# High and low parts of a 16-column weight side by side in one stationary tile

## The chip, the cores and the metric

The program runs on one core of a Trainium2 chip. The metric is the device time of one execution in microseconds (us), less is better. The core's engines work side by side, each through its own instructions in order: TensorE (PE in the rows; PEld are its weight loads), VectorE (DVE), ScalarE (ACT), GpSimd (POOL) and SyncE (SP, which here issues most transfers).

## The reference, cut to what matters

One inference step of a two-layer network for 640 tokens (128 of a prompt, 512 of a sample), all in float32. Each layer feeds a normalised input `h` to four token mixers, merges their outputs through gates, and ends with a feed-forward part. The first mixer is a gated delta rule. Its log decay `g` and write strength `beta` come from 16 columns of the input projection, 8 for the decay and 8 for the strength (2 directions x 4 heads):

```
aq, ak, av, az, aa, ab, ... = split(h @ w_in)           # aa, ab: 8 columns each
g    = -exp(a_log) * softplus(aa + dt_bias)
beta = sigmoid(ab)
o, state = chunked delta rule(q, k, v, g, beta, s0)
```

## The kernel before, in words

Activations stand with the features on the partitions and the 640 tokens along the row, in two halves of 320. To keep float32 accuracy, a matrix product of weights W and activations X is made from parts in the type fp32r: W = Wh + Wl and X = Xh + Xl, and the product is Wh Xh + Wh Xl + Wl Xh. `load_w` loads a weight tile (`wraw`), copies it to its high part `whi` on ScalarE and subtracts on VectorE to get the low part `wlo`. `unit` then makes one product for one half of the tokens: 8 blocks of 128 features, three matmuls each, summed in one PSUM bank `pu`. The activations' parts are `hh` and `hl`.

`a_small` is the projection to the 16 columns: one `load_w` of 128 columns (8 blocks of 16) and two `unit`s with M=16, that is 48 matmuls, whose result goes to `ab` (16 partitions x 640 tokens). `a_small2` turns `ab` with five PE transposes into `pabt` (tokens on the partitions), copies that to `abt` and computes decay and strength from it; `peg` are its small float32 matmuls.

The order of the work in the mixer stage of a layer is made by a planner in the program (`weave`). It has chains (the mixers, `prep_a`, `prep_b`, in a fixed order of rank) and fill (`a_small` first, then the other projections `store_fm` and `store_tok`, pregates and merges). It keeps a modelled clock, `self.now`, which each matmul moves on by its modelled cost; a chain's next step is put into PE's queue as soon as the modelled time of what it waits for, plus a margin, has come, and fill is put in between. PE keeps exactly that order. The orders of the other engines come from priorities and from the order in which the instructions were written.

Names in the rows: `cacc`, `craw` are the short convolution of `prep_a` (VectorE, six instructions a time); `pkS`, `xp`, `vn`, `pao` belong to the delta rule; `cY`, `cZ`, `cQS`, `cRP`, `pca`, `pcb`, `cAT` to the seven levels of `mix_c`, in which VectorE makes `cY` and `cZ` and PE multiplies them into `pca` and `pcb`; `rx`, `rr`, `rot` to the rotation in `prep_b`; `stg`, `sth` are the results of `store_fm` and their high parts on the way out to memory; `lmr`, `lmn` a small scalar of `mix_b`. `stg` and `sth` share six buffers, and three PSUM banks hold the fill's `pu`.

Of the kernel before, what the change touches and what calls it, by code (L numbers as in the profile page):

```python
# [8 lines left out]
F32 = mybir.dt.float32  # L9
F32R = mybir.dt.float32r  # L10
I32 = mybir.dt.int32
ACT = mybir.ActivationFunctionType
ALU = mybir.AluOpType
# [5 lines left out]
HT = T // 2  # L19
# [49 lines left out]
def bc1(ap, n):  # L69

    d = [list(x) for x in ap.ap]
    return bass.AP(tensor=ap.tensor, offset=ap.offset, ap=[d[0], [0, n]] + d[1:])
# [40 lines left out]
class Net:  # L113
# [600 lines left out]

    def a_small(self, l):

        w = self.load_w(self.I['wab'][l], 128)
        ab = self.S("ab")
        for j in range(2):
            ps = yield from self.unit(w, self.h, range(8), j, M=16)  # L720
            self.a.copy(ab[:16, j * HT:(j + 1) * HT], ps[:16, :HT])
        self.abT = ab
        self.ev['ab'] = self.now

    def a_small2(self, l):

        v, a = self.v, self.a
        yield 'ab',
        ab = self.abT
        yield ab,  # L730
        pt = self.M("pabt")
        for t in range(5):
            self.tp(pt[:, t * 16:(t + 1) * 16], ab[:16, t * 128:(t + 1) * 128], self.ident[:16, :16])
        abt = self.Q("abt", 80)
        v.tensor_copy(abt, pt[:, :80])
        abv = abt.rearrange("p (t c) -> p t c", t=5)
        f = lambda n: self.Q(n, 40)
        u, e, w1, r, d = f("a_u"), f("a_e"), f("a_w"), f("a_r"), f("a_d")
        q = lambda t: t.rearrange("p (t c) -> p t c", t=5)
        v.tensor_tensor(q(u), abv[:, :, 0:8], bc1(self.dtb[:, l, :], 5), ALU.add)  # L740
        a.activation(e, u, ACT.Abs)
        a.activation(e, e, ACT.Exp, scale=-1.0)
        v.tensor_scalar(w1, e, 1.0, None, ALU.add)
        a.activation(r, w1, ACT.Ln)
        v.tensor_scalar(d, w1, -1.0, 1e-30, ALU.add, ALU.max)
        v.reciprocal(d, d)
        v.tensor_tensor(r, r, e, ALU.mult)
        v.tensor_tensor(r, r, d, ALU.mult)
        v.scalar_tensor_tensor(u, u, 0.0, r, ALU.max, ALU.add)
        g = self.sm("a_g", 40)  # L750

        gv = g.rearrange("p (d t h) -> p t d h", d=2, t=5)
        ea = self.sm("a_ea", 8)
        a.activation(ea, self.alog[:, l, :], ACT.Exp)
        v.tensor_scalar(ea, ea, -1.0, None, ALU.mult)
        for dr in range(2):
            v.tensor_tensor(gv[:, :, dr], q(u)[:, :, dr * 4:dr * 4 + 4], bc1(ea[:, dr * 4:dr * 4 + 4], 5), ALU.mult)
        be = self.sm("a_b", 40)
        bv = be.rearrange("p (d t h) -> p t d h", d=2, t=5)
        for dr in range(2):  # L760
            a.activation(bv[:, :, dr], abv[:, :, 8 + dr * 4:12 + dr * 4], ACT.Tanh, scale=0.5)
        v.tensor_scalar(be, be, 0.5, 0.5, ALU.mult, ALU.add)
        yield g,
        pe = self.M("peg")
        for i, (m, dr) in enumerate(((self.Ui, 0), (self.Ls, 0), (self.ones, 0), (self.Li, 1), (self.Us, 1), (self.ones, 1))):
            self.mm(pe[:, i * 20:(i + 1) * 20], m, g[:, dr * 20:(dr + 1) * 20], start=True, stop=True)
        eg = self.sm("a_eg", 120)
        a.activation(eg, pe[:, :120], ACT.Exp)
        ng = self.sm("a_ng", 120)
        v.tensor_scalar(ng, eg, -1.0, None, ALU.mult)  # L770
        self.g_, self.be, self.eg, self.ng = g, be, eg, ng
# [1183 lines left out]
```

## Time and profile before

| | |
|---|---|
| median of 3 runs | 3432.06 us (3429.37 to 3438.22) |
| profiled execution: its own time | 3430.03 us |
| its span, first to last instruction | 3428.3 us |
| PE busy | 3344.3 us, 98% of the span, 23932 matmul records |
| VectorE, ScalarE, GpSimd busy | 68%, 41%, 6% |
| granted PE clock, mean | 0.992 of full speed |

PE is busy nearly all the time; its matmuls overlap, so their step (from one start to the next) tells their cost, not the mean duration. Two other things can lengthen the time: moments in which PE stands still, and stretches in which its clock is granted at less than full speed.

### The profile page before, as it was taken

The numbers are of one execution on the slowest core, as the hardware profiler recorded it, in microseconds if no ns is written. First come the engines' busy times: TensorE is split into PE (matmuls) and PEld (weight loads), VectorE is DVE, ScalarE is ACT, GpSimd is POOL, SyncE is SP. The second block draws the span as 40 slices with busy tenths as digits, with TensorE's granted clock in tenths as the row PEclk, the third lists the DMA queues.
The fourth block names the chain that finished last, engine by engine and source line by source line (L and its number), as shares of the span: only waits on it lengthen the run. The fifth ranks groups of instructions, "written<-read, shape, count | busy, mean of one in ns | idle before, by whom it ended". The sixth has DMA issues, their size and how long they took to land. (4 is left out here: it accounts for less than half of the span.)

```text
span 3428.3 us, 62644 instructions
## 1 busy us (share of the span) xinstructions
PE 3344.3 (98%) x23932; PEld 3279.3 (96%) x23932; DVE 2315.9 (68%) x5237; ACT 1420.5 (41%) x3166; POOL 215.6 (6%) x385
## 2 busy tenths in 40 slices
PE   8999999999999999999999999999999999999998
PEld 5999999999999999999999999999999999999998
DVE  7689888876675577887456898777555656634335
ACT  5354545554443352222253455455444433422222
POOL 1000001210010000000001010012010100000000
PEclk9999999999999999999999999999999999999999
DMA  6544334865453444544234432348444325322222
GB/s 220 161 154 137 122 118 143 241 192 175 130 148 100 132 155 145 154 151 134 79 124 145 146 121 99 112 135 238 143 150 137 104 82 169 100 72 76 75 80 68
DMA packets 288133, 460.10 MB, mean 134 GB/s; under 512 B 47061, under 2 KB 174677, under 8 KB 287833
## 3 DMA queue, kind: packets, MB, share of 16 engines
q1 hardware_dynamic: 276504, 423.58, 39.5%
q0 software_dynamic: 11328, 32.52, 3.2%
q8 instruction: 189, 3.10, 0.4%
q14 instruction: 112, 0.91, 0.1%
HBM read 368.42 MB, written 87.56 MB: 133 GB/s over the span
## 5 line engine op out<-in xcount | busy, mean ns | idle before, releaser
L151 PE MATMUL pu<-hh,whi 128*128 128x320 f32 (+1 forms) x3760 | 1090.7, 318 | 12.9 <-ACT stg L106 9.7
L151 PE MATMUL pu<-hl,whi 128*128 128x320 f32 (+1 forms) x3760 | 1061.8, 310 | 2.4 <-DVE hl L106 2.4
L151 PE MATMUL pu<-hh,wlo 128*128 128x320 f32 (+1 forms) x3760 | 1062.4, 310 | 0.0
L106 ACT CAST whi<-wraw 128x1024 fp32r<-128x1024 f32 (+2 forms) x410 | 390.4, 952 | 884.8 <-PE pu L151 562.4
L151 PEld LDWEIGHTS pu<-hh,whi 128*128 128x128 f32 (+1 forms) x3760 | 681.3, 188 | 17.7 <-ACT stg L106 10.5
L151 PEld LDWEIGHTS pu<-hl,whi 128*128 128x128 f32 (+1 forms) x3760 | 681.3, 188 | 4.5 <-DVE hl L106 2.6
L151 PEld LDWEIGHTS pu<-hh,wlo 128*128 128x128 f32 (+1 forms) x3760 | 680.0, 188 | 1.7
L106 DVE TENSOR_TENSOR wlo<-wraw,whi 128x1024 fp32r<-128x1024 f32 (+2 forms) x410 | 455.4, 1111 | 311.7 <-ACT whi L106 302.7
L151 PE MATMUL pu<-mo,whi 128*128 128x320 f32 x1024 | 233.9, 316 | 3.8 <-ACT mo L106 1.9
L151 PE MATMUL pu<-fa,whi 128*128 128x320 f32 x1152 | 215.6, 309 | 0.0
L106 DVE SCALAR_TENSOR_TENSOR x<-pu,gn,x 128x128 f32<-128x128 f32 (+1 forms) x336 | 134.0, 434 | 92.8 <-PE pu L151 91.8
L151 PE MATMUL ptk<-whi,hh 128*128 128x256 f32 x640 | 191.1, 299 | 0.0
L151 PE MATMUL ptk<-wlo,hh 128*128 128x256 f32 x640 | 181.1, 283 | 1.2 <-DVE wlo L106 1.2
L151 PE MATMUL ptk<-whi,hl 128*128 128x256 f32 x640 | 181.2, 283 | 0.0
L151 PEld LDWEIGHTS pu<-fa,whi 128*128 128x128 f32 x1152 | 180.8, 188 | 0.0
L151 PEld LDWEIGHTS pu<-mo,whi 128*128 128x128 f32 x1024 | 172.1, 190 | 5.8 <-DVE mo L106 3.1
L151 PE MATMUL pu<-mo,wlo 128*128 128x320 f32 x512 | 159.5, 311 | 0.0
L151 PE MATMUL pu<-fa,wlo 128*128 128x320 f32 x576 | 131.2, 309 | 0.0
L511 DVE CUSTOM_DVE_ANT_0 junk<-wa,cs,bada 128x512 bf16<-128x512 f32 x160 | 119.6, 747 | 7.1 <-DMA wa<-in_wada 4.8
L511 DVE CUSTOM_DVE_ANT_0 junk<-wa,cs,mod 128x512 bf16<-128x512 f32 x160 | 119.5, 747 | 7.0 <-DMA wa<-in_wada 4.6
L151 PEld LDWEIGHTS ptk<-wlo,hh 128*128 128x128 f32 x640 | 122.4, 191 | 1.4 <-DVE wlo L106 1.4
L106 DVE TENSOR_TENSOR fs<-fs,pu 128x320 f32<-128x320 f32 x88 | 39.6, 483 | 124.3 <-PE pu L151 124.3
(422 smaller groups left out, 5967.1 us busy)
## 6 DMA issues: line engine op xcount, KB each, us to landing
wraw<-in_win SPq DMA_DIRECT2D x151, 512.0 KB, 3.7
wa<-in_wada SPq DMA_DIRECT2D x180, 256.0 KB, 3.0
wraw<-in_wg SPq DMA_DIRECT2D x44, 512.0 KB, 3.5
wraw<-in_wu SPq DMA_DIRECT2D x44, 512.0 KB, 3.5
wraw<-in_wd SPq DMA_DIRECT2D x80, 256.0 KB, 2.6
p<-stg SPq DMA_DIRECT2D x112, 160.0 KB, 2.7
wraw<-in_wtok SPq DMA_DIRECT2D x32, 512.0 KB, 3.8
wraw<-in_wbr SPq DMA_DIRECT2D x32, 512.0 KB, 3.5
```

Source lines behind the costliest of these rows:

```text
L106: r = f(*args, **kw)
L151: r = self.nc.tensor.matmul(out, lhsT, rhs, start=start, stop=stop)
L511: self.nc.vector.tensor_tensor_reduce(junk, raw, cs[g], 0.5, o if k0 else self.bada[:, l, m:m + 1], ALU.mult, ALU.add, o)
```

## The change

`a_small` no longer makes two tiles. It copies the 8 blocks of 16 columns to places 0 to 15 of 32 columns per block, and writes the low part of the same block into places 16 to 31. A matmul with this 32-column tile gives the high part's product in 16 rows of the result and the low part's in 16 others, so that one block needs two matmuls (`hh` and `hl`) where it needed three; the product Wl Xl is now made too. `ab` has 32 partitions. `a_small2` builds a 32 x 16 matrix `two` (two identity matrices on top of each other) and replaces each transpose by a float32 matmul with it, which transposes and adds the two halves. The cast and the subtraction no longer have the raised priority that `load_w` gives them, and no `wlo` buffer is taken.

```diff
     def a_small(self, l):

-        w = self.load_w(self.I['wab'][l], 128)
+        raw = self.wraw.tile([128, 1024], F32, tag="raw", name="wraw")[:, :128].rearrange("p (k c) -> p k c", c=16)
+        self.nc.sync.dma_start(raw, self.I['wab'][l].rearrange("p (k c) -> p k c", c=16))
+
+        w = self.whl.tile([128, 1024], F32R, tag="hi", name="whi")[:, :256].rearrange("p (k c) -> p k c", c=32)
+        self.a.copy(w[:, :, :16], raw)
+        self.v.tensor_tensor(w[:, :, 16:], raw, w[:, :, :16].bitcast(F32), ALU.subtract)
         ab = self.S("ab")
         for j in range(2):
-            ps = yield from self.unit(w, self.h, range(8), j, M=16)
-            self.a.copy(ab[:16, j * HT:(j + 1) * HT], ps[:16, :HT])
+            ps = self.G1("pu")
+            c = slice(j * HT, (j + 1) * HT)
+            for k in range(8):
+                for i in range(2):
+                    self.mm(ps[:32, :HT], w[:, k], self.h[k][i][:, c], start=k == 0 and i == 0, stop=k == 7 and i == 1)
+                yield ()
+            self.a.copy(ab[:32, c], ps[:32, :HT])
...
         ab = self.abT
-        yield ab,
+        two = self.Q("two", 16)[:32]
+        v.tensor_tensor(two, self.ident[:32, :16], self.ident[:32, 16:32], ALU.add)
+        yield ab, two
         pt = self.M("pabt")
         for t in range(5):
-            self.tp(pt[:, t * 16:(t + 1) * 16], ab[:16, t * 128:(t + 1) * 128], self.ident[:16, :16])
+            self.mm(pt[:, t * 16:(t + 1) * 16], ab[:32, t * 128:(t + 1) * 128], two, start=True, stop=True)
```

In each layer PE's queue loses 16 matmuls. Because the planner's modelled clock is earlier by their cost from there on, it puts many later steps into PE's queue with a few matmuls of fill more or fewer between them. The three places below are those that matter for what follows.

Place 1 is PE in layer 0, the end of `a_small`; the fill behind it is the next `store_fm`. Before, the last rows with 16 columns and the transposes:

```order
L151 MATMUL pu<-hh,whi 16x320
L151 MATMUL pu<-hl,whi 16x320
L151 MATMUL pu<-hh,wlo 16x320
L151 MATMUL pu<-hh,whi 128x320
L151 MATMUL pu<-hl,whi 128x320
L151 MATMUL pu<-hh,wlo 128x320
L157 MATMUL pabt<-cst_119,ab 128x16 x5
```

The same place after the change:

```order
L151 MATMUL pu<-hh,whi 32x320
L151 MATMUL pu<-hl,whi 32x320
L151 MATMUL pu<-hh,whi 128x320
L151 MATMUL pu<-hl,whi 128x320
L151 MATMUL pu<-hh,wlo 128x320
L151 MATMUL pabt<-two,ab 128x16 x5
```

One matmul of three is gone from each block, 48 rows of this kind have become 32 in each layer; `pabt` stands as many rows behind them as it did.

Place 2 is VectorE in layer 1, first head of `mix_c`, the rows that end with the `cZ` of the sixth level. Before:

```order
L106 SCALAR_TENSOR_TENSOR cacc<-craw,convw,cacc 128x642
L106 SCALAR_TENSOR_TENSOR SS<-SS,a_eg,pkS 128x128
L106 SCALAR_TENSOR_TENSOR cacc<-craw,convw,cacc 128x642
L106 SCALAR_TENSOR_TENSOR xp<-pkS,a_ng,avt 128x128
L106 SCALAR_TENSOR_TENSOR cacc<-craw,convw,cacc 128x642
L106 SCALAR_TENSOR_TENSOR xp<-pkS,a_ng,avt 128x128
L106 TENSOR_TENSOR cY<-cY,cK 128x640
L106 TENSOR_SCALAR vn<-pkS,a_b 128x128 x2
L106 SCALAR_TENSOR_TENSOR cacc<-craw,cacc 128x642
L106 TENSOR_TENSOR wlo<-wraw,whi 128x1024
L106 TENSOR_TENSOR cZ<-cZ,cq 128x640
```

After the change the rows that end with the same `cZ` are these:

```order
L106 TENSOR_SCALAR ars_y<-ars_t 128x5
L106 SCALAR_TENSOR_TENSOR xp<-pkS,a_ng,avt 128x128
L106 SCALAR_TENSOR_TENSOR ars_t<-ars_y 128x5
L106 TENSOR_TENSOR GX<-GX,pX 128x4x2x64
L106 TENSOR_TENSOR ars_t<-ars_t,ams 128x5
L106 SCALAR_TENSOR_TENSOR xp<-pkS,a_ng,avt 128x128
L106 SCALAR_TENSOR_TENSOR ars_y<-ars_t,ars_y 128x5
L106 TENSOR_TENSOR cY<-cY,cK 128x640
L106 TENSOR_TENSOR ars_t<-ars_y,ams 128x5
L106 COPY_PREDICATED cAT<-cst,pca 128x512
L106 SCALAR_TENSOR_TENSOR ars_t<-ars_t,ars_y 128x5
L106 TENSOR_TENSOR cZ<-cZ,cq 128x640
```

Between the fifth level's `cZ` and this one there stood six convolution rows and three `wlo` of 1024 columns; now there is neither.

Place 3 is VectorE in layer 1, where `mix_b` begins and four `stg` wait for their low part (`stg<-stg,sth`). Before:

```order
L106 TENSOR_TENSOR cZ<-cZ,cq 128x640
L106 TENSOR_TENSOR cRP<-cRP 128x10x2x32
L106 TENSOR_TENSOR cY<-cY,cK 128x640
L106 TENSOR_TENSOR cQS<-cQS,cRP 128x5x2x64
L106 TENSOR_TENSOR lmn<-lmr 128x1
L106 TENSOR_TENSOR rx<-rx,rr 128x2x512
L106 TENSOR_TENSOR wlo<-wraw,whi 128x1024
L106 TENSOR_TENSOR cQS<-cQS,cK 128x640 x2
L106 TENSOR_SCALAR lmn<-lmn 128x1
L106 TENSOR_TENSOR stg<-stg,sth 128x192
L106 TENSOR_TENSOR stg<-stg,sth 128x320
L106 TENSOR_TENSOR stg<-stg,sth 128x192
```

After the change:

```order
L106 TENSOR_REDUCE lmr<-lmp 128x2
L106 TENSOR_TENSOR rr<-rr,rot 128x2x512
L106 TENSOR_TENSOR lmn<-lmr 128x1
L106 TENSOR_TENSOR stg<-stg,sth 128x320
L106 TENSOR_SCALAR lmn<-lmn 128x1
L106 TENSOR_TENSOR rx<-rx,rr 128x2x512
L106 TENSOR_TENSOR stg<-stg,sth 128x192
L106 TENSOR_TENSOR stg<-stg,sth 128x320
L106 TENSOR_TENSOR rx<-rx,rr 128x2x512
L106 TENSOR_TENSOR stg<-stg,sth 128x192
L106 COPY_PREDICATED cAT<-cst,pca 128x512
L106 COPY_PREDICATED cAT<-cst,pcb 128x128
```

The four subtractions stood behind the last levels of `mix_c` and now stand ahead of two more of them.

## Rows read from the trace of the kernel before

**Rows 1.** The page: span, and busy time of PE.

```profile
span 3428.3 us, 62644 instructions
PE 3344.3 (98%) x23932; PEld 3279.3 (96%) x23932; DVE 2315.9 (68%) x5237; ACT 1420.5 (41%) x3166; POOL 215.6 (6%) x385
```

**Rows 2.** Timeline of PE, layer 0: start us, duration us, instruction, [idle before].

```profile
69.00 0.31 PE L151 MATMUL pu<-hh,whi 128*128 128x320 f32 x1
...
69.89 0.31 PE L151 MATMUL pu<-hh,whi 128*16 128x320 f32 x1
70.03 0.30 PE L151 MATMUL pu<-hl,whi 128*16 128x320 f32 x1
...
76.92 0.32 PE L151 MATMUL pu<-hh,whi 128*128 128x320 f32 x1
...
77.46 0.48 PE L157 MATMUL pabt<-cst,ab 16*128 16x16 f32 x5
77.88 0.41 PE L151 MATMUL pu<-hh,whi 128*128 128x320 f32 x1
```

**Rows 3.** Weight loads by tile: minimum/median/maximum ns, and forms.

```profile
L151 PEld LDWEIGHTS pu<-hh,whi x3760: 94/188/337, 40.4 to 3368.4; 128*128 128x128 f32 x196, 128*16 128x16 f32 x2
L151 PEld LDWEIGHTS peg<-a_g,cst x24: 187/192/192, 86.7 to 1796.8; 128*128 128x128 f32 x24
```

**Rows 4.** Timeline of PE, layer 0: the six float32 matmuls of 20 columns.

```profile
86.89 1.41 PE L151 MATMUL peg<-a_g,cst 128*128 128x20 f32 x12
88.14 0.39 PE L151 MATMUL pu<-hh,whi 128*128 128x320 f32 x1
```

**Rows 5.** Timeline of VectorE: start of the program, and the low part in each layer.

```profile
3.00 0.17 DVE L106 TENSOR_SCALAR a_b<-bada 128x8 f32<-128x8 f32 x1 [3.00 <-DMA bada<-in_bada]
...
68.97 0.29 DVE L106 TENSOR_TENSOR wlo<-wraw,whi 128x128 fp32r<-128x128 f32 x1
...
1760.65 0.29 DVE L106 TENSOR_TENSOR wlo<-wraw,whi 128x128 fp32r<-128x128 f32 x1 [0.91 <-ACT whi L106]
```

**Rows 6.** Timeline of PE, layer 1: first 16-column product, and the transposes.

```profile
1777.86 0.31 PE L151 MATMUL pu<-hh,whi 128*16 128x320 f32 x1
...
1786.37 0.35 PE L157 MATMUL pabt<-cst,ab 16*128 16x16 f32 x3 [0.64 <-ACT ab L106]
```

**Rows 7.** Whom PE waited for: us in total, times, longest.

```profile
PE pu L151 <- ACT stg L106: 9.7, 3, 6.9
PE pca L151 <- DVE cZ L106: 8.0, 2, 4.4
```

**Rows 8.** Timeline around the longest pause: VectorE, ScalarE, PE.

```profile
2349.05 1.02 DVE L106 TENSOR_TENSOR stg<-stg,sth 128x192 fp32r<-128x192 f32 x3
2349.43 0.44 ACT L106 ACTIVATE stg<-pu 128x320 f32<-128x320 f32 x1 [2.81 <-DVE stg L106]
2349.92 0.63 PE L151 MATMUL pu<-hh,whi 128*128 128x320 f32 x1 [6.95 <-ACT stg L106]
```

**Rows 9.** Timeline around the second pause: VectorE, PE.

```profile
2014.07 0.83 DVE L106 SCALAR_TENSOR_TENSOR cacc<-craw,cacc 128x642 f32<-128x642 f32 x1 [0.30 <-ACT craw L106]
2014.81 1.22 DVE L106 TENSOR_TENSOR wlo<-wraw,whi 128x1024 fp32r<-128x1024 f32 x1
2015.95 1.67 DVE L106 TENSOR_TENSOR cZ<-cZ,cq 128x640 f32<-128x640 f32 x1
2017.76 2.04 PE L151 MATMUL pca<-cZ,cY 128*128 128x128 f32 x8 [4.42 <-DVE cZ L106]
```

**Rows 10.** Windows behind pauses: busy us of each engine, then PEclk, DMA share, GB/s.

```profile
2350.00:2356.00 6.00, 6.00 (x26) 6.00 (x27) 1.44 (x4) 1.93 (x7) 2.86 (x6) 0.53 1.03 282
2018.00:2024.00 6.00, 6.00 (x37) 5.99 (x38) 6.00 (x9) 2.34 (x8) 2.25 (x2) 0.74 0.16 61
656.00:660.00 4.00, 4.00 (x21) 4.00 (x20) 4.00 (x8) 3.64 (x8) 0.00 (x0) 0.60 1.07 287
```

**Rows 11.** Timeline of VectorE, layer 0: its longest wait at the rotation.

```profile
652.86 1.23 DVE L106 TENSOR_TENSOR rx<-rx,rot 128x1024 f32<-128x1024 f32 x1 [8.72 <-issue]
```

## The prediction, made before the changed kernel ran

> **What bounds the kernel.** I read the page first: PE is busy for 3344.3 of 3428.3 us [rows 1], so what PE has to do, and where it stands still, sets the end; the other engines matter only where PE waits for them. Then PE's timeline around `a_small`: its 48 products of 16 columns per layer run without a gap among the products of 128 columns, in the same step [rows 2]. They are on the path, each at its full step. Then the list of whom PE waited for [rows 7]. Few waits are long; the two longest are one of 6.9 us for an `stg` of ScalarE and one of 4.4 us for a `cZ` of VectorE. The timelines of those places [rows 8, 9] say what was late, and windows just behind them [rows 10] show the granted clock: 0.53 over 6 us after the first, 0.74 over 6 us after the second, so that PE, having stood still, worked for some us at the lower level of 1.2 GHz. A pause costs more than its own length.
>
> **The products.** In layer 0 the 48 products start at 69.89 us and the next 128-column product at 76.92 us [rows 2]: 7.03 / 48 = 0.1465 us each. The six 128-column products before them take (69.89 - 69.00) / 6 = 0.148 us each, so the number of columns in the stationary tile doesn't show in the step, and 32 should cost what 16 and 128 do. Sixteen fewer in each of two layers: 32 x 0.1465 = 4.7 us less. The bound on the other side: nothing in the rows lets a 32-column product be slower than a 128-column one, which would be 64 x 0.0015 = 0.1 us.
>
> The weight loads of `pu` take 94 to 337 ns, median 188 [rows 3], longer than the step, and the short loads of the 16-column tiles bring no shorter step: the loads lie under the matmuls. A rule of the Trainium skill (TensorE: Matmul & The Clock Gate, Part 3, The mechanism) speaks against that: a load overlaps with matmuls under way only where it goes to other row groups, and all tiles here fill all 128 rows. With that page's load time of columns / 1.2 ns (section on LDWEIGHTS), an estimate would be that each of the 64 remaining products has 13 ns more to load, 0.9 us in all. The equal steps don't agree with that rule.
>
> **The transposes.** Five transposes take from 77.46 to 77.88 us, 0.084 us each [rows 2]. Their place is taken by five float32 matmuls of 16 columns, a kind that the trace doesn't have in this shape. Nearest are the six `peg`, float32 with 20 columns: 86.89 to 88.14 us, 0.209 us each [rows 4], because each is recorded as two loads and two matmuls (24 loads for twelve of them, [rows 3]). Bounds: 0.084 and 0.209 us. I take the upper one, since the shape is almost the same: 10 x (0.209 - 0.084) = 1.25 us more in two layers. The Trainium skill (FP8 and Floating Point Precision, TensorE Precision Notes) says that true float32 takes four passes; the rows show two records each, and with twice the price the whole count would save some 1.3 us instead of 3.4.
>
> **What is hidden.** The low part is now written with stride into the same tile, and as all 32 columns are read at once, the first product must wait for it. In layer 0 it was ready at 68.97 + 0.29 = 69.26 us [rows 5] and the first product started at 69.89: 0.63 us of cover, over twice the instruction's length. If the strided write doubled its time, the first product would still not wait; if the cover were gone, it would cost at most 0.3 us, once. In layer 1 the cover is from 1760.94 to 1777.86 us [rows 5, 6]. Both instructions have kept their places in their queues although they lost priority. `two` costs a VectorE instruction of 0.17 us like `a_b` [rows 5]; in layer 0 it is VectorE's first, ahead of `a_b`, which waits until 3.00 us for a transfer that SyncE issues after the one `two` needs. The copies of `ab` have the same length along the row. In layer 1 the last transposes waited 0.64 us for `ab` [rows 6]; their place behind it is kept, so I let that wait stay, and bound it by 0 and 0.64. The chain behind `a_small` (decay, strength, `peg`) starts some 2 us earlier relative to the fill; PE has fill to do all the while, so nothing comes of that by itself.
>
> So the count alone gives 4.7 - 1.25 = 3.4 us less. Against the profiled execution's own time, 3430.0, that is 3426.6.
>
> **What is moved.** The planner's clock is 16 products earlier in each layer, and with that the rows of every engine in the mixer stages are shuffled a little. That is a change of PE's pauses, not of its work. The two longest pauses are the ones to look at.
>
> The longest: the fill's product waited 6.95 us for a PSUM bank; ScalarE could not empty it because it had no free `stg` buffer, as the `stg` ahead waited on VectorE for their subtraction, which began only at 2349.05 us [rows 8]. Place 3 shows why: they stood behind the last levels of `mix_c`, `rx` and a `wlo`. After the change four of them stand ahead of the next two levels. Price of the pause with the slower clock after it: 6.95 + 6 x 0.47 = 9.8 us.
>
> The second: `pca` waited 4.42 us because VectorE had the convolution and a `wlo` ahead of `cZ` [rows 9]. In place 2 both are gone from between these two levels. Price: 4.42 + 6 x 0.26 = 6.0 us.
>
> Bounds of what the two give back: 0 and 15.8 us. A row order says who stands ahead, not when an input comes, so I take six tenths, 9.4 us. New pauses must come up elsewhere from the same shuffle: bounds 0 and another 15.8; I take one of the third size, the other wait for `cZ`, 8.0 - 4.4 = 3.6 us [rows 7], with 4 x 0.40 = 1.6 us of clock behind it [rows 10]: 5.2 us. Sum: 3426.6 - 9.4 + 5.2 = 3422.4 us; I say **3422**. The profiled execution is 2 us under the median of the runs, 3432.06. A change of 0.3%, about what a measurement of this kernel can tell from none, is 10.3 us: below 3421.8 or above 3442.4.
>
> **The rivals.**
>
> *Only the count.* New pauses cost what the old ones did: 3426.6. For it: the pauses are many, most of them short, and a shuffle removes as readily as it adds. Against it: places 2 and 3. Chance 0.25.
>
> *Both pauses go and nothing comes up*: 3426.6 - 15.8 = 3410.8. For it: the same places; against it: every one of the later rows is moved, and none of those moves was chosen for its waits. Chance 0.14.
>
> *Slower, by VectorE standing at the rotation.* VectorE waits in its queue for a transfer at `rx`, the longest time 8.72 us [rows 11], and the levels of `mix_c` behind it wait too. Where the shuffle puts `rx` ahead of a level that PE needs at once, PE stands for up to 8.72 us, and with 2.8 us of clock as after the longest pause that is 11.5 us. One such more gives 3438, no difference that shows; it decides from two on: 3426.6 + 23 = 3450. Eight `rx` in the two layers could do it. Against it: in the rows of before the wait of 8.72 us cost PE only the 3.6 us one. Chance 0.09.
>
> *The count doesn't arrive*: 32-column products or the float32 ones cost so much more that nothing is saved: 3430. The equal steps speak against it. Chance 0.07.
>
> **How the numbers follow.** The forecast has 0.45, with its own range 3416 to 3428. It lies at the border of 0.3%, so half of it counts as faster. Faster: 0.22 + 0.14 + 0.04 of "only the count" = 0.40. Slower: 0.08 of the rotation's 0.09. Same: 0.52. The range 3409 to 3438 takes in the case without the two pauses and a single new long one, and leaves out the two-fold rotation and the far end of the best case, together under 2 in 10.
>
> **What would show it.** Right: 32 products in 4.7 us per layer between the neighbours; `pabt` in about 1.05 us; the wait of `pu` for `stg` well under 6.9 us and that of `pca` for `cZ` under 4.4 us; and the sum of PE's pauses smaller by some us. Wrong: a step over 0.15 us for the 32-column products; a gap ahead of the first of them; a new pause over 5 us, above all with VectorE waiting at `rx`; or windows with a granted clock near 0.5 in places that had 1.0.

## The result and the profile after

The changed kernel takes 3456.28 us (median of 6 runs, 3443.23 to 3461.32) against 3432.62 us (6 runs of the kernel before beside them): ratio 1.0065, 95% interval 1.0050 to 1.0081. It is slower by 24 us. The forecast was 3422, the range ended at 3438: the prediction was wrong, in sign too.

The profiled execution took 3453.77 us, 23.7 us more than that of before. The page of the changed kernel, to be read beside [rows 1]:

```profile
span 3452.0 us, 62597 instructions
PE 3354.9 (97%) x23910; PEld 3290.6 (95%) x23910; DVE 2315.5 (67%) x5239; ACT 1413.8 (41%) x3162; POOL 214.6 (6%) x385
```

PE has 22 matmul records fewer (32 products less, 10 records of `pabt` more) and is busy 10.6 us longer. That looks like a contradiction, until the granted clock is read with it: 0.988 as a mean, where it was 0.992. A rough split of the span follows from three numbers of each page. Time in which PE stands still is the span less PE's busy time: 84.0 us before, 97.1 after, 13.1 more. Time lost to the clock is at most span x (1 - clock): 27.4 and 41.4 us, 14 more (the clock has three digits, so each of the two is known to 1.7 us). What is left, PE's work at full clock, is 3316.9 and 3313.5: 3.4 us less. That it is just the 3.4 of the count is luck: in the profiles of the experiments below the same sum gives 3308 to 3317 for kernels with the changed kernel's very work. So the split says that the loss lies in pauses and in the clock; the saving of the count has to be read from PE's timeline.

That is, in layer 0, against [rows 2]:

```profile
66.80 0.30 PE L151 MATMUL pu<-hh,whi 128*32 128x320 f32 x1
66.94 0.30 PE L151 MATMUL pu<-hl,whi 128*32 128x320 f32 x1
...
71.49 0.32 PE L151 MATMUL pu<-hh,whi 128*128 128x320 f32 x1
...
72.60 1.28 PE L151 MATMUL pabt<-two,ab 32*128 32x16 f32 x10 [0.50 <-ACT ab L106]
73.81 0.41 PE L151 MATMUL pu<-hh,whi 128*128 128x320 f32 x1
```

The 32 products take from 66.80 to 71.49 us, 0.1466 us each where the 16-column ones took 0.1465. No gap stands ahead of the first. The weight loads of the 32-column tiles are recorded with 108 ns (median), those of the 16-column ones with 95, and the step doesn't show the difference. The estimate of 13 ns more for each product, by the rule of the Trainium skill (TensorE: Matmul & The Clock Gate, Part 3, The mechanism) with the load time of its section on LDWEIGHTS, is not borne out in the step. `pabt` takes 1.21 us to the next start, 0.242 us for each of the five, a little over the upper bound of 0.209; it waited 0.50 us for `ab`.

Now the waits. Whom PE waited for in the changed kernel (us in total, times, longest), against [rows 7]:

```profile
PE pco L151 <- DVE cSS L106: 9.3, 4, 3.7
PE pu L151 <- ACT stg L106: 9.0, 3, 4.8
PE pca L151 <- DVE cZ L106: 8.1, 2, 4.5
...
PE pcs L151 <- ACT ckd L106: 2.8, 2, 2.5
...
PE pat L157 <- DVE a_ea L106: 2.6, 1, 2.6
```

The two rows on which the gain was built (`pu` for `stg`, `pca` for `cZ`) stand nearly as before in their totals, 9.0 and 8.1 us where they were 9.7 and 8.0, and new names have come up. PE's timeline shows where (in the brackets the pause, and who ended it):

```profile
85.43 1.30 PE L157 MATMUL pat<-cst,cacc 128*128 128x128 f32 x5 [2.55 <-DVE a_ea L106]
...
609.92 0.38 PE L151 MATMUL pcs<-cv,ckd 128*128 128x128 f32 x1 [2.46 <-ACT ckd L106]
656.20 2.07 PE L151 MATMUL pca<-cZ,cY 128*128 128x128 f32 x8 [4.50 <-DVE cZ L106]
680.45 0.63 PE L151 MATMUL pu<-hh,whi 128*128 128x320 f32 x1 [3.82 <-ACT stg L106]
...
960.00 0.44 PE L157 MATMUL pds<-cst,dP 128*128 128x128 f32 x2 [2.53 <-ACT dP L106]
1993.02 1.72 PE L151 MATMUL pca<-cZ,cY 128*128 128x128 f32 x8 [3.58 <-DVE cZ L106]
...
2014.48 1.06 PE L151 MATMUL pca<-cZ,cY 128*128 128x128 f32 x8
...
2049.32 0.79 PE L151 MATMUL pco<-cSS,cRP 128*128 128x128 f32 x2 [3.26 <-DVE cSS L106]
2171.37 0.80 PE L151 MATMUL pco<-cSS,cRP 128*128 128x128 f32 x2 [3.65 <-DVE cSS L106]
2345.86 0.63 PE L151 MATMUL pu<-hh,whi 128*128 128x320 f32 x1 [4.76 <-ACT stg L106]
```

The reader is to see many pauses of 2.5 to 5 us, of different names and in both layers, and no single culprit. The row at 2014.48 is the sixth level of `mix_c` in the first head of layer 1, place 2 of the change: its wait of 4.42 us [rows 9] is gone, and the 3.58 us at 1993.02 are a new wait of the same kind two levels earlier. Over the whole timeline pauses of 2 us and more were 11, together 39.2 us, and are 17, together 54.7 us. Windows around three of the new ones (busy us of each engine, PEclk, DMA share, GB/s):

```profile
84.00:92.00 8.00, 6.57 (x28) 6.60 (x29) 2.38 (x11) 2.79 (x14) 0.16 (x3) 0.58 0.20 68
2046.00:2056.00 10.00, 6.74 (x34) 6.68 (x34) 4.81 (x10) 4.77 (x13) 1.98 (x3) 0.66 0.44 136
2170.00:2178.00 8.00, 6.63 (x45) 6.64 (x46) 2.70 (x7) 3.26 (x13) 1.17 (x1) 0.79 0.63 190
```

The granted clock was 0.58, 0.66 and 0.79 there, that is, a good part of each window at 1.2 GHz. In the first, 0.42 x 8 = 3.4 us are lost to the clock behind a pause of 2.55 us. PE's busy time grows with it, which is why it went up while its work went down.

### The profile page after: what moved, and what is told of

The parts are those of the page before. It is cut to its first block, busy times and chain, and to the rows that moved or that the text cites. A ratio compares the mean times of both kernels' runs of the same rounds, so it can differ in the third digit from the quotient of the medians.

```text
span 3452.0 us, 62597 instructions
## 1 busy us (share of the span) xinstructions
PE 3354.9 (97%) x23910; PEld 3290.6 (95%) x23910; DVE 2315.5 (67%) x5239; ACT 1413.8 (41%) x3162; POOL 214.6 (6%) x385
## 4 chain that ended last, share of the span: by engine, by line
PE 79%; DVE 9%; DMA 5%; issue 3%; ACT 3%; SPq 1%; POOL 1%; DVEq 0%; ACTq 0%; POOLq 0%
PE pu L151 58%; PE ptk L151 4%; PE pdv L151 2%; PE pbs L151 1%; PE pbo L151 1%; PE pW L151 1%; PE pca L151 1%; PE pX L151 1%; PE pT L151 1%; DVE cacc L106 1%; DMA craw<-p 1%; PE pdt L157 1%; PE pds L151 1%; DVE wlo L106 1%; PE pkS L151 1%
## 5 line engine op out<-in xcount | busy, mean ns | idle before, releaser
L151 PE MATMUL pu<-hh,wlo 128*128 128x320 f32 x3728 | 1054.9, 311 | 0.0
L151 PEld LDWEIGHTS pu<-hh,wlo 128*128 128x128 f32 x3728 | 678.8, 189 | 0.1
L106 DVE SCALAR_TENSOR_TENSOR x<-pu,gn,x 128x128 f32<-128x128 f32 (+1 forms) x336 | 133.6, 434 | 91.5 <-PE pu L151 90.9
L151 PEld LDWEIGHTS ptk<-whi,hh 128*128 128x128 f32 x640 | 122.8, 192 | 0.0
```

The lines of the kernel that those rows point to most:

```text
L106: r = f(*args, **kw)
L151: r = self.nc.tensor.matmul(out, lhsT, rhs, start=start, stop=stop)
```

## The experiments

Two theories were put against each other. *Order*: the planner's clock is earlier, so PE's queue has another order in both mixer stages, and that order has more pauses. *Work*: the wide products, the float32 matmuls or the lost priority cost more than they look. Every kernel was compared with runs of the kernel before on the same chip. What is added to the modelled clock in experiments 1 to 8 changes the order of the program and nothing that it computes.

**1. The new work in the order of before.** Each step of two products moves the modelled clock as three did, and `pabt` as the transposes did:

```diff
                     self.mm(ps[:32, :HT], w[:, k], self.h[k][i][:, c], ...)
+                self.now += HT / 2.4 + 3
...
+        self.chain = False
         v.tensor_tensor(two, self.ident[:32, :16], self.ident[:32, 16:32], ALU.add)
+        self.chain = True
...
             self.mm(pt[:, t * 16:(t + 1) * 16], ab[:32, t * 128:(t + 1) * 128], two, ...)
+            self.now -= (384 - 64) / 2.4
+            self.t[pt.tensor.name] = self.now + 160
```

> The new products, the float32 matmuls and the lost priority are all in; only the planner's modelled clock is put back to what it was before, so that PE's queue has the order of before. Theory 'order' (the later rows' new order makes the loss): 3432.6 - 3.4 = 3429 us, ratio 0.999. Rival 'work' (the 32-column products, the float32 matmuls or the lost priority of cast and subtraction make it): 3456 us, ratio 1.007.

Measured: 3431.39 us, ratio 0.9994 (0.9984 to 1.0004). The new work alone is not slower; *work* falls. Its page:

```profile
span 3429.6 us, 62603 instructions
PE 3344.6 (98%) x23910; PEld 3281.8 (96%) x23910; DVE 2316.3 (68%) x5239; ACT 1421.3 (41%) x3166; POOL 215.2 (6%) x385
```

Pauses 85.0 us and clock 0.991, nearly as before. Even here most of what the count saves in layer 0 is given back a little later, at `pat`, which transposes the result of the convolution `cacc`. First the kernel before, then experiment 1:

```profile
85.46 0.71 PE L157 MATMUL pat<-cst,cacc 128*128 128x128 f32 x5
```

```profile
68.44 0.30 PE L151 MATMUL pu<-hh,whi 128*32 128x320 f32 x1
...
74.94 0.41 PE L151 MATMUL pu<-hh,whi 128*128 128x320 f32 x1
...
83.68 0.74 PE L157 MATMUL pat<-cst,cacc 128*128 128x128 f32 x5 [1.00 <-DVE a_ea L106]
```

From the first narrow product to the row behind `pabt` PE took 8.0 us before (77.88 - 69.89, [rows 2]) and 6.5 here: 1.5 us saved. It came to `pat` after 15.6 us before (85.46 - 69.89) and after 14.2 here (83.68 - 1.00 - 68.44), 1.3 us sooner; then it waited 1.00 us, and 0.3 us were left. (`a_ea` is the row that VectorE ran right behind the convolution; what `pat` reads is `cacc`.)

**2. The old work in the new order.** The reverse: the kernel before, its clock moved back at each step of the 16-column products and on at each transpose.

```diff
-            ps = yield from self.unit(w, self.h, range(8), j, M=16)
+            gen = self.unit(w, self.h, range(8), j, M=16)
+            try:
+                while True:
+                    next(gen)
+                    self.now -= HT / 2.4 + 3
+                    yield ()
+            except StopIteration as s:
+                ps = s.value
...
             self.tp(pt[:, t * 16:(t + 1) * 16], ab[:16, t * 128:(t + 1) * 128], self.ident[:16, :16])
+            self.now += (384 - 64) / 2.4
+            self.t[pt.tensor.name] = self.now + 160
```

> The kernel before with its 48 products, its transposes and its priorities; only the modelled clock is moved by what the change moved it, so that PE's queue has the order of the changed kernel. Theory 'order': 3456.3 + 3.4 = 3460 us, ratio 1.008. Rival 'work': 3433 us, ratio 1.000.

Measured: 3447.75 us, ratio 1.0039 (1.0026 to 1.0051), where 3460 was expected. Not one instruction is changed, only the order, and the kernel is 13 us slower (by the ratio; 15 by the medians). The order is a cause by itself. But it is not the whole: this kernel has 3.4 us more work than the changed one and should have been slower than that, and is 9 us faster.

**3 and 4. The new order in one layer alone.** The additions of experiment 1 are multiplied by `(l == 1)` or `(l == 0)`, so that layer 0 alone, or layer 1 alone, keeps the new order.

> The changed kernel with the modelled clock put back in layer 1 alone: layer 0 has the new order, layer 1 that of before. By the two traces layer 0's mixer stage lost 5.7 us although 16 products were gone (1178.6 against 1172.9 us at its end), so some 7.5 us are the order's. Theory 'order': 3429 + 7.5 = 3437 us, ratio 1.001. Rival 'work': 3456 us.

Measured: 3441.18 us, 1.0017 (1.0005 to 1.0028).

> The changed kernel with the modelled clock put back in layer 0 alone: layer 1 has the new order. From the start of layer 1's mixer stage to the last stage the changed kernel lost 16.8 + 3.5 = 20.3 us, some 20 us the order's. Theory 'order': 3429 + 20 = 3449 us, ratio 1.005. Rival 'work': 3456 us.

Measured: 3441.18 us, 1.0027 (1.0012 to 1.0042). Against experiment 1 each layer's order costs some 10 us by the medians, 8 and 11 us by the ratios. For layer 0 that agrees with the 7.5 us that the two traces had given, within its uncertainty; layer 1 weighs less than the 20 us expected. Their sum, 3431.4 + 9.8 + 9.8 = 3451, is within the uncertainty of the 3456.3 measured.

**5 to 8. Other orders of the same work.** Is the new order an unlucky one, or that of before an unusually good one? Experiment 1's kernel with one more line in `a_small`, which shifts the modelled clock in both layers:

```diff
+        self.now += -700
         self.abT = ab
         self.ev['ab'] = self.now
```

and with 700, 1500 and 3000 (ns) in its place.

> The kernel of the first experiment (new products, order of before) with the modelled clock moved by -0.7 us at the end of a_small in both layers: 174 rows of PE's queue move, a ninth of what the change moved. Theory 'the order of before is an unusually good one': with so few rows moved the time stays near it, 3430 to 3436 us, ratio 0.999 to 1.001. Rival 'the new order was an unlucky one of many alike': 3424 to 3436 us, on either side.

> As the last with +0.7 us: 1320 rows of PE's queue move, nearly as many as in the change. Theory 'unusually good': it loses as the change did, 3440 to 3460 us, ratio 1.003 to 1.008. Rival 'unlucky': 3420 to 3440 us, a ratio on either side of 0.999.

> As the last with +1.5 us (the change's own distance, to the other side): 1698 rows of PE's queue move. Theory 'unusually good': 3440 to 3460 us. Rival 'unlucky': 3420 to 3440 us; of the last three kernels at least one at or under 3429 us.

> As the last with +3 us: 1953 rows of PE's queue move. Theory 'unusually good': 3440 to 3460 us. Rival 'unlucky': 3420 to 3440 us.

Measured: 3428.03 (0.9984, 0.9974 to 0.9993), 3442.41 (1.0037, 1.0025 to 1.0050), 3447.72 (1.0047, 1.0031 to 1.0064) and 3446.34 us (1.0049, 1.0030 to 1.0067). All three large shuffles lose 10 to 15 us against the kernel before, 11 to 16 against experiment 1, which does the same work; none gains. The small one stays near, at 3428.0 a little faster than the 3430 to 3436 that the theory gave. With the changed kernel's own that makes four thoroughly different orders, all slower. "Unusually good" holds, for the order of before and those close to it. By its median the changed kernel's order, 25 us above experiment 1, is the worst of the four as well, though its interval overlaps those of experiments 7 and 8.

**9. The priority alone.** The cast and the subtraction of `a_small` get their raised priority back:

```diff
-        self.a.copy(w[:, :, :16], raw)
-        self.v.tensor_tensor(w[:, :, 16:], raw, w[:, :, :16].bitcast(F32), ALU.subtract)
+        with self.tc.high_priority(offset=WPRI):
+            self.a.copy(w[:, :, :16], raw)
+            self.v.tensor_tensor(w[:, :, 16:], raw, w[:, :, :16].bitcast(F32), ALU.subtract)
```

> The changed kernel with the raised priority given back to a_small's cast and subtraction, one part of the change alone. No queue's order differs from that of the changed kernel by more than the branch row. Theory 'order': no effect, 3456 us, ratio 1.0065. Rival 'lost priority makes a part of the loss': under 3450 us.

Measured: 3455.81 us, 1.0066 (1.0052 to 1.0080). No effect. As it has the same rows in the same order, it is the changed kernel measured once more.

**10. The saved products done all the same.** In the changed kernel each block gets a third 32-column product into a bank `px` that nobody reads, and the modelled clock is not moved by it:

```diff
-            ps = self.G1("pu")
+            ps, px = self.G1("pu"), self.M("px")
...
+                self.mm(px[:32, :HT], w[:, k], self.h[k][0][:, c], start=k == 0, stop=k == 7)
+                self.now -= HT / 2.4 + 3
```

> The changed kernel with the 16 spared products per layer done all the same (32-column products whose sum, in a bank px, nobody reads), modelled clock and order of the other PE rows as in the changed kernel; on VectorE the first convolution row of layer 0 is ahead of a wlo again, as in the kernel with the old products. Theory 'the saved products only bring PE earlier to a chain that is not ready' (the pause of 2.55 us of pat for a_ea at 85.43 us and the lower clock behind it): 4.7 us more work cost nothing, 3448 to 3456 us, and the pause at pat is gone. Rival 'work is work': 3456 + 4.7 = 3461 us.

Measured: 3446.43 us, 1.0037 (1.0024 to 1.0049), even below the 3448 to 3456 of the theory. With 4.7 us more work the kernel is not slower but 9 us faster than its twin in experiment 9. The place that the expectation named, PE's timeline and a window of this kernel:

```profile
69.19 0.30 PE L151 MATMUL pu<-hh,whi 128*32 128x320 f32 x1
...
87.57 0.77 PE L157 MATMUL pat<-cst,cacc 128*128 128x128 f32 x5 [0.54 <-DVE cacc L106]
```

```profile
84.00:92.00 8.00, 7.46 (x55) 7.20 (x54) 4.79 (x16) 5.74 (x17) 0.16 (x3) 1.00 0.53 173
```

The pause of 2.55 us is 0.54 and the clock 1.00 instead of 0.58. VectorE's timeline shows what `pat` waited for; first the kernel before, then the changed kernel, then experiment 10 (first and last row of the convolution):

```profile
78.73 0.55 DVE L106 TENSOR_SCALAR cacc<-craw,convw 128x642 f32<-128x642 f32 x1 [1.24 <-DMA craw<-p]
...
84.27 0.82 DVE L106 SCALAR_TENSOR_TENSOR cacc<-craw,cacc 128x642 f32<-128x642 f32 x1
```

```profile
75.18 0.18 DVE L106 TENSOR_SCALAR a_d<-a_w 128x40 f32<-128x40 f32 x1
76.78 1.23 DVE L106 TENSOR_TENSOR wlo<-wraw,whi 128x1024 fp32r<-128x1024 f32 x1 [1.41 <-ACT whi L106]
77.92 0.55 DVE L106 TENSOR_SCALAR cacc<-craw,convw 128x642 f32<-128x642 f32 x1
...
84.45 0.83 DVE L106 SCALAR_TENSOR_TENSOR cacc<-craw,cacc 128x642 f32<-128x642 f32 x1 [0.82 <-ACT craw L106]
85.20 0.16 DVE L106 TENSOR_SCALAR a_ea<-a_ea 128x8 f32<-128x8 f32 x1
```

```profile
79.11 0.56 DVE L106 TENSOR_SCALAR cacc<-craw,convw 128x642 f32<-128x642 f32 x1 [3.21 <-DMA craw<-p]
...
86.69 0.83 DVE L106 SCALAR_TENSOR_TENSOR cacc<-craw,cacc 128x642 f32<-128x642 f32 x1 [1.00 <-ACT craw L106]
```

All times from the first narrow product:

| | convolution begins | it ends | PE comes to `pat` |
|---|---|---|---|
| before | 8.8 us | 15.2 | 15.6 |
| changed | 11.1 | 18.5 | 16.1 |
| experiment 10 | 9.9 | 18.3 | 17.8 |

In the changed kernel the convolution ended 3.3 us later than in the kernel before, and PE came only 0.5 us later. Rows of `a_small2`, among them `a_d`, and a `wlo` for which VectorE waited 1.41 us stood ahead of its first row. In experiment 10, as in experiment 2, that row stands ahead of the `wlo` again; but in experiment 10 its last row ends as late as in the changed kernel. What took the pause away is that PE comes 1.8 us later: the extra products fill the wait. Which of VectorE's rows make the convolution late was not separated. At this place the extra products gain 2.0 us of pause and 3.4 us of clock, 5.4 us for 4.7 us spent in both layers. That explains why they cost nothing, not why the kernel gains 9; with the uncertainty of both ratios the 9 us may be 3 to 16.

**11 and 12. Seven buffers for `stg`.** `NGS = 7` instead of 6, in the changed kernel and in that of experiment 5; PE's order is the same row by row.

> The changed kernel with seven buffers for stg and sth instead of six; PE's order is the same row by row. The two pauses of pu for stg were 4.8 and 3.8 us, each with 6.8 us of half clock behind. Theory 'pauses and the clock behind them make the loss': without the two, 3456.3 - 8.6 - 6.8 = 3441 us, if others don't grow. Rival 'a pause taken away comes back elsewhere': 3450 to 3456 us.

Measured: 3452.99 us, 1.0053 (1.0041 to 1.0066), as the rival had it.

> The kernel with the clock at -0.7 us (new products, nearly the order of before) and seven buffers. Its pause of pu for stg was 5.36 us at 2344.42. Theory 'pauses and clock': 3428.0 - 5.4 - 3.4 = 3419 us, ratio 0.996. Rival 'comes back elsewhere': 3428 us, ratio 0.998.

Measured: 3426.84 us, 0.9980 (0.9971 to 0.9989). Here too the rival's forecast is the near one. The pauses didn't go (two of `pu` for `stg`, 3.9 and 4.3 us, in experiment 11, one of 5.88 in 12), so the prices were not put to the test. Timelines of experiment 12, ScalarE, VectorE and PE:

```profile
2347.18 0.28 ACT L106 ACTIVATE stg<-pu 128x128 f32<-128x128 f32 x1 [1.35 <-DVE stg L106]
```

```profile
2346.67 1.15 DVE L106 TENSOR_TENSOR stg<-stg,sth 128x320 fp32r<-128x320 f32 x3
```

```profile
2347.72 0.64 PE L151 MATMUL pu<-hh,whi 128*128 128x320 f32 x1 [5.88 <-ACT stg L106]
```

ScalarE's copy out of the PSUM bank again stood still until VectorE had made its subtractions of `stg`. One more buffer doesn't help where VectorE comes late. Still, this kernel and that of experiment 5 are the fastest of all: 0.2% under the kernel before, 0.8% under the changed one.

All kernels together, with the profiled execution's own time, pauses and clock:

| kernel | median us | profiled us | span less PE busy | clock |
|---|---|---|---|---|
| before | 3432.6 | 3430.0 | 84.0 | 0.992 |
| 1, new work, old order | 3431.4 | 3431.4 | 85.0 | 0.991 |
| 5, clock -0.7 us | 3428.0 | 3428.4 | 84.1 | 0.991 |
| 12, the same, 7 buffers | 3426.8 | 3429.0 | 83.6 | 0.991 |
| 3, new order in layer 0 | 3441.2 | 3442.3 | 94.7 | 0.989 |
| 4, new order in layer 1 | 3441.2 | 3439.1 | 89.2 | 0.991 |
| 2, old work, new order | 3447.8 | 3435.9 | 89.1 | 0.991 |
| 10, 48 products | 3446.4 | 3448.7 | 92.8 | 0.990 |
| 6, clock +0.7 us | 3442.4 | 3439.0 | 90.9 | 0.991 |
| 7, clock +1.5 us | 3447.7 | 3450.0 | 95.1 | 0.989 |
| 8, clock +3 us | 3446.3 | 3446.9 | 97.6 | 0.991 |
| changed | 3456.3 | 3453.8 | 97.1 | 0.988 |
| 9, priority back | 3455.8 | 3445.9 | 95.6 | 0.990 |
| 11, changed, 7 buffers | 3453.0 | 3456.2 | 97.9 | 0.987 |

The last two columns belong to one execution each. For experiments 2 and 9 that was their fastest, 12 and 10 us under the median, so these two rows may show less than the usual loss. The four kernels with the order of before or one near it have 84 to 85 us of pauses; all others have 89 to 98.

## Why the prediction was wrong

**The count was right.** 0.1466 us for each wide product, no wait ahead of the first, `two` and the strided low part hidden: as predicted. `pabt` was a little dearer, 1.21 us where 1.05 was taken. Experiment 1 has the count alone at 3431, no measurable change; the prediction had 3426.6 for that case, counted from an execution 2 us under the median. The interval of experiment 1 reaches 5 us under the kernel before, so it neither shows nor excludes the 3.4 us. In layer 0, where the count saved 1.5 us up to the end of `pabt`, 0.3 were left at `pat`. The two other doubts, wide products and lost priority, are excluded by experiments 1 and 9.

**The step that failed is "What is moved".** It took the reshuffle of the queues for a chance to lose pauses: six tenths of the two longest gone, 9.4 us (0.6 x 15.8 is 9.5), and one new one for 5.2 us, together 4.2 us of gain. The reshuffle alone costs 13 us (experiment 2). The places that it looked at did get better: at place 2 the 4.42 us are gone, and near place 3, three units of the fill earlier, PE waited 4.76 us where it had waited 6.95. The error lies on the other side: new pauses came at places that the prediction did not price, two of them of the same kinds (3.58 us of `pca` for `cZ` two levels earlier, 3.82 us of `pu` for `stg` in layer 0), so that the totals of both kinds stayed, 8.1 and 9.0 us. In all there are 17 pauses of 2 us and more instead of 11. The prediction looked closely at the two worst places of an order with few bad ones. Such places can hardly get worse, while all the good ones can; looking there could hardly show anything but a gain. From experiments 6 to 8 a fair estimate of a large reshuffle of this program would have been +11 to +16 us, and with it 3438 to 3443: the right side, and still 13 us or more short of the 3456 measured.

**A sentence under "What is hidden" failed too**: that the chain behind `a_small` starts 2 us earlier relative to the fill and nothing comes of it, since PE has fill to do. In the new order its rows and a `wlo` stood ahead of the convolution on VectorE, which ended 3.3 us later, and `pat` waited 2.55 us at 85.43. Experiment 10 shows that at this place the saved products bought nothing.

**The rivals.** *Only the count* is what experiment 1 makes of the change, not what the change does. The rival on the slower side had the right side and the right kind of cause (VectorE not yet there when PE comes), and the wrong place: of the pauses shown, only that of `pca` at 656.20 stands behind a wait at `rx` of 8.53 us as in [rows 11] (now put down to the transfer `rx<-qk`, which the row of before did not name), and PE waited 4.5 us there where it had waited 3.6. The new ones are of `cSS`, `ckd`, `dP` and `a_ea`, besides those of `stg` and `cZ` above. At 2049.32 VectorE had five rows of a convolution, 0.6 to 0.9 us each, ahead of the states `cSS`:

```profile
2042.51 0.56 DVE L106 TENSOR_SCALAR cacc<-craw,convw 128x642 f32<-128x642 f32 x1 [0.62 <-DMA craw<-p]
...
2047.11 0.88 DVE L106 SCALAR_TENSOR_TENSOR cacc<-craw,convw,cacc 128x642 f32<-128x642 f32 x1
2047.90 0.34 DVE L106 SCALAR_TENSOR_TENSOR ao<-ao,grs_y,z 128x128 f32<-128x128 f32 x1
2048.17 1.10 DVE L106 SCALAR_TENSOR_TENSOR cSS<-cSS,cfl,pcs 128x128 f32<-128x128 f32 x3
```

That is read from the trace; no experiment moved these rows alone.

**What stays open.** That the order of before is better than four others is shown as a fact, not explained. The modelled clock moves rows in the queues of several engines at once, and no experiment moved one engine's queue alone. And of the 9 us by which experiments 2 and 10 beat the changed kernel, some 5 us before the price of the added products lie at `pat`; the rest was not located.

## What to carry to other kernels

Where a planner derives a queue's order from a modelled clock, an edit that saves work also moves the clock, and with it everything behind: keep the two apart by measuring the new work in the old order first, and then look for an order. When a reshuffle has to be priced from one trace, don't price the worst pauses of the order at hand; a good order has more to lose than to gain, and each new pause costs its length and often some us of lower clock behind it. Work that is saved just ahead of a chain with a latency of its own (here transfer, convolution, transpose) is largely given back as a wait there: 1.0 of 1.3 us in experiment 1.

## What the runs showed of the hardware

Runs of one program differ by about as much as this change is worth: 33 runs of the kernel before on one chip reach from 3422.10 to 3446.71 us. The clock goes with it: the six runs of the changed kernel reach from 3443.23 us, with a mean granted clock of 0.990, to 3461.32 us, with 0.987. At 3450 us a difference of 0.003 is 10 of the 18 us. A short pause was enough to lose the clock: 2.55 us of standing still in the changed kernel, and 0.58 granted over the 8 us around it.
